# A two-way hybrid layer (2-D attention and mLSTM): all large SBUF tiles start at multiples of 64 bytes

## The chip, the cores and the metric

The kernel runs on one core of one Trainium2 chip. The metric is the device time of one execution in microseconds (us). TensorE multiplies matrices (PE in the profile, its weight loads PEld), VectorE (DVE) and ScalarE (ACT) work elementwise, GpSimd (POOL) fills constants and does small steps, SyncE (SP) issues most of the DMA transfers. SBUF is the on-chip memory: 128 partitions, in each of which a tile takes the same range of bytes. Where that range starts is what this change is about.

## The reference

One layer of a bidirectional encoder on 1,280 tokens (a prompt of 1,024 and a sample of 256) of 2,048 features, in fp32:

```python
hn = rmsnorm(x, norm_w)
proj = jnp.einsum('btd,dp->btp', hn, w_in)            # 2048 -> 9232 columns
# group A: 8 heads of neighbourhood attention over a grid 64 wide
att = neighbourhood_attention(q, k, v, rpb) * silu(na_g)
# group B: conv + SiLU on q and k, 4 heads of a chunkwise mLSTM in both directions
h = bidirectional_mlstm(silu(conv(mq)), silu(conv(mk)) * d**-0.5, mv, gates)
mem = rmsnorm(h, head_norm_w) * sigmoid(ml_o) * silu(ml_z)
y = rmsnorm(x + concat([att, mem]) @ w_out, final_norm_w)
```

## The kernel before

Every large fp32 matrix product is made of three matmuls: each operand is split into a rounded part hi and a rest lo (the helper `split`, lines 178 to 187: ACT casts hi, DVE subtracts for lo), and hi x hi, hi x lo and lo x hi are summed in PSUM. On top of this the projections and the out-projection use schemes with seven block products where a plain one has eight, so sums of blocks are formed on DVE and POOL ahead of them.

The work goes through these stages, with their place in the profiled execution:

- 0 to 1090 us, group A of the tokens (768 of them): `first_tiles` loads and splits x, then `pair_a` projects pairs of 128 columns with matmuls of 384 columns (`mm_c`, line 288; moving tiles xb and xg, weights such as A22s), and `unit_vg` makes v and gate columns (line 499).
- 1090 to 1365 us, group B (512 tokens): `proj_v` (line 777, 256 columns, the moving tile is the split weight wsv and the split x tiles x_0h, x_0l and so on are the stationary weights), the gates, and ten runs of `pair_s` (line 1416, 256 columns, 7 steps each of 8 x 3 matmuls; moving are x tiles in the steps 1, 2, 3 and block sums xs in the steps 6, 5, 4, 7; the weights S32s and the like come from the pool wb for the first half of each step and from xs2 for the second).
- 1365 to 2150 us, attention (lines 807 to 956, scores 810, transposes through ident 827, weights times v 923, 932, 938) and mLSTM (lines 1093 to 1330, matmuls 1132), interleaved with the rest of `proj_pair` (line 694, 512 columns, moving x, weights ws) and `proj_v`.
- 2150 to 2540 us, the out-projection `product` (line 1684, 512 columns, moving wo or wt, weights mo), the residual and the final norm (lines 1604 to 1668).

The tiles come from pools. A pool hands out one ring of equal slots per tag. Pools that are opened on the left grow up from the low end of SBUF (const, then xa and wa for group A; later late, xp1, xs2, and ap or "att" with mp), pools with `side="right"` grow down from the high end (xr for group A; later wb, xp0). A tile's size is rounded up to 32 bytes, and pools follow each other without gaps. So a pool's start depends on the sizes of all that was opened on its side before it. Before the change the constants take a number of bytes that is 32 past a multiple of 64, and the high end lies 32 past one as well. Most slots have sizes that are multiples of 64, so nearly everything starts at 32 of 64. The exceptions are five tags with an odd size in 32 bytes: po (520 floats, 2,080 bytes, six slots in wb, lines 657 to 658), sc (520, line 1385), sml (260, 1,040 bytes, line 802), and kvf and cb (516, line 1135). Their slots alternate between 0 and 32. Each of these tiles is used through views that are narrower than or as wide as the tile.

The order on each engine is not written by hand everywhere. A scheduler with an estimated timeline of its own sets it from priorities and from when slots come free; in the interleaved stage, where several streams are ready at once, small differences of its estimate change which stream's instruction comes next.

Of the kernel before, what the change touches and what calls it, by code (L numbers as in the profile page):

```python
# [9 lines left out]
F32 = mybir.dt.float32  # L10
F32R = mybir.dt.float32r
# [3 lines left out]
P = 128  # L15
# [14 lines left out]
NRA, NWS, NWT, NPC, NPO = 3, 8, 4, 5, 6  # L30
# [18 lines left out]
def kernel(  # L49
# [17 lines left out]
    nc = tc.nc  # L67
    V, S, G, PE, DM = nc.vector, nc.scalar, nc.gpsimd, nc.tensor, nc.sync

    const = ctx.enter_context(tc.tile_pool(name="const", bufs=1))  # L70
    dram = ctx.enter_context(tc.tile_pool(name="spill", bufs=1, space=bass.MemoryType.DRAM))
    ps = ctx.enter_context(tc.tile_pool(name="ps", bufs=3, space=bass.MemoryType.PSUM))

# [95 lines left out]
    def x_split(raw, k, g):  # L169
        h, l = x_pair(k, f"x{g}_{k}")  # L170
        S.mul(h, raw, lnw_sb[:, k : k + 1])
        V.scalar_tensor_tensor(
            l, raw, lnw_sb[:, k : k + 1], f(h), op0=ALU.mult, op1=ALU.subtract
        )
        return h, l
# [458 lines left out]
    for i, n1 in enumerate(order):  # L634
# [4 lines left out]
        k = i - 4  # L639
# [7 lines left out]
    wb, xp0 = pools  # L647
# [7 lines left out]
    xp1 = ctx.enter_context(tc.tile_pool(name="xp1", bufs=1))  # L655

    def po(name):
        return wb.tile([P, 520], F32, tag="po", name=name, bufs=NPO)

    def w_piece(src, name):  # L660
        raw = wb.tile([P, 1024], F32, tag="wraw", name=f"wr_{name}", bufs=2)
# [12 lines left out]
    def conv_b(o, ct):  # L674
        cv = po(f"pcv{ct}")
        yield from conv_taps(cv, o, ct, 516, 0)
        hi = wb.tile([P, 520], F32R, tag="po", name=f"pch{ct}", bufs=NPO)
        store_conv(ct, cv, hi, o, ((0, 258, GA - 2), (260, 516, TP)))

    FORTH = ((0, 1), (0, 0), (1, 0))  # L680
# [1 line left out]
    def proj_pair(n1, X, late=False):  # L682
        pb = [bank("pr", f"pc{n1}_{j}") for j in range(2)]
        for r in range(4):
            raw = w_piece(w_in[n1 // 2, r], f"{n1}_{r}")
            t = [w_split(raw, j * 512, j * 512 + 512, f"{n1}_{r}{j}") for j in range(2)]
            for f_ in range(2):
                for q in range(2):
                    xs = X.get(8 * f_ + 2 * r + q)
                    c = (2 * f_ + q) * P  # L690
                    first, last = r + f_ + q == 0, r == 3 and f_ == 1 and q == 1
                    for j, passes in enumerate((FORTH, FORTH[::-1])):
                        for m, (wi, xi) in enumerate(passes):
                            PE.matmul(  # L694
                                pb[j], t[j][:, wi, c : c + P], xs[xi],
                                start=first and m == 0, stop=last and m == 2,
                            )
        out = []
        for j in range(2):
            o = po(f"pco{n1}_{j}")  # L700
            if QK0 <= n1 < OT0:
                ct = n1 - QK0 + j
                DM.dma_start(o[:, 0:4], qb[ct])
                for z in (260, 518):
                    G.memset(o[:, z : z + 2], 0.0)
                out_scaled(
                    o[:, 4:].rearrange("p (s c) -> p s c", s=2)[:, :, :256],
                    pb[j].rearrange("p (s c) -> p s c", s=2),
                    rbs[1].rearrange("p (s c) -> p s c", s=2), n1,
                )  # L710
                for _ in conv_b(o, ct):
                    pass
                continue
            o = o[:, :GB]
            out_scaled(o, pb[j], rbs[1], n1)
            if n1 < GT0:
                store_qk(
                    n1 + j, o,
                    lambda dt: wb.tile([P, 520], dt, tag="po", name=f"ps{n1}_{j}_{dt}", bufs=NPO),
                    PARTS_B,  # L720
                )
            elif not late:
                DM.dma_start(pT[n1 + j][:, GA:], o)
            out.append(o)
        return out
# [20 lines left out]
    def proj_v(u, X):  # L746
        gates = u == NA_H // 2
        w = 272 if gates else 256
        nt = GB // P
        if gates:  # L750
            outs = [bank("a", f"pv{u}_{i}")[:, :w] for i in range(nt)]
        else:
            pb = [bank("pr", f"pv{u}_{i}") for i in range(nt // 2)]
            outs = [pb[t // 2][:, (t % 2) * 256 : (t % 2) * 256 + 256] for t in range(nt)]
        for r in range(4):
            raw = w_piece(w_in[NCH // 2 + u, r], f"v{u}_{r}")
            rawv = raw.rearrange("p (j f q c) -> p f q j c", j=2, f=2, q=2)
            if gates:
                graw = wb.tile([P, 2, 2, 16], F32, tag="wgr", name=f"wg{r}", bufs=2)
                DM.dma_start(  # L760
                    graw, w_g.rearrange("p (f r q c) -> p f r q c", f=2, r=4, q=2)[:, :, r]
                )
            for f_ in range(2):
                t = wb.tile([P, 2, 544], F32R, tag="wsp", name=f"wsv_{u}_{r}_{f_}", bufs=4)
                t4 = t[:, :, : 2 * w].rearrange("p h (k c) -> p h k c", k=2)
                h2, l2 = (
                    t4[:, z, :, 0:256].rearrange("p q (j c) -> p q j c", j=2) for z in range(2)
                )
                split(h2, l2, rawv[:, f_])
                if gates:  # L770
                    split(t4[:, 0, :, 256:272], t4[:, 1, :, 256:272], graw[:, f_])
                for tt in range(nt):
                    for q in range(2):
                        first, last = r + f_ + q == 0, r == 3 and f_ == 1 and q == 1
                        xh, xl = X.get(8 * f_ + 2 * r + q)
                        for m, (xs, wi) in enumerate(((xh, 0), (xh, 1), (xl, 0))):
                            PE.matmul(  # L777
                                outs[tt],
                                xs[:, tt * P : (tt + 1) * P],
                                t[:, wi, q * w : (q + 1) * w],  # L780
                                start=first and m == 0 and (gates or tt % 2 == 0),
                                stop=last and m == 2 and (gates or tt % 2 == 1),
                            )
        rc = rcs[1]
        for tt in range(nt):
            o = wb.tile([P, 520], F32R, tag="po", name=f"vo{u}_{tt}", bufs=NPO)
            o = o[:, :512].rearrange("p (a d) -> p a d", a=2)
            store_v(u, GA + tt * P, o, outs[tt][:, :256], rc[:, tt : tt + 1])
            if gates:
                V.scalar_tensor_tensor(  # L790
                    gt[:, GA // P + tt, :], outs[tt][:, 256:272], rc[:, tt : tt + 1], gb_sb,
                    op0=ALU.mult, op1=ALU.add,
                )
# [5 lines left out]
        return ap.tile([P, 512], dt, tag="mid", name=name, bufs=6)[:, :n]  # L799

    def sml(name, n=256, dt=F32):
        return ap.tile([P, 260], dt, tag="sml", name=name, bufs=6)[:, :n]

    def na_tile(tag, shape, name, bufs, dt=F32):
        return ap.tile(shape, dt, tag=tag, name=name, bufs=bufs)
# [287 lines left out]
    def ml_units(sq, h, gates):  # L1093
# [38 lines left out]
                PE.matmul(o, lhs(a_), rhs(b_), start=first and m == 0, stop=last and m == 2)  # L1132

        def kvt(name, tag="kvf", bufs=4):
            t = ap.tile([P, 516], F32, tag=tag, name=name, bufs=bufs)
            return t.rearrange("p (t c) -> p t c", c=VW)

        def c_split(name, src):
# [193 lines left out]
    class LazyX:  # L1332
# [2 lines left out]

        def get(self, k):
            if k not in self.t:
                self.t[k] = x_split(x_raw(wb, 520, "po", NPO, 1, k), k, 1)
            return self.t[k]

    def run(*streams):
# [37 lines left out]
    def pair_s(n1, tag, bg):  # L1379
# [2 lines left out]
        x0, y0, z0, y1, z1 = bx[:, :256], by[:, :256], bz[:, :256], by[:, 256:], bz[:, 256:]  # L1382
        conv = QK0 <= n1 < OT0
        off = (4, 262) if conv else (0, 256)
        Cn = [xs2.tile([P, 520], F32, tag="sc", name=f"{nm}c0", bufs=2), po(f"{nm}c1")]
        c0, c1, c2, c3 = (Cn[j][:, o : o + 256] for j in range(2) for o in off)
        steps = (
            (1, x0, True), (2, y0, True), (6, x0, False), (5, z0, True), (3, z1, False),
# [62 lines left out]
    def finish_s(n1, Cn):  # L1451
        for j, o in enumerate(Cn):
            if QK0 <= n1 < OT0:
                ct = n1 - QK0 + j
                DM.dma_start(o[:, 0:4], qb[ct])
                for z in (260, 518):
                    G.memset(o[:, z : z + 2], 0.0)
                yield from conv_b(o, ct)
                continue
            o = o[:, :GB]  # L1460
            if n1 < GT0:
                store_qk(
                    n1 + j, o,
                    lambda dt: wb.tile([P, 520], dt, tag="po", name=f"S{n1}_{j}_{dt}", bufs=NPO),
                    PARTS_B,
                )
                yield
                continue
            if OT0 <= n1 < ZT0:
                S.activation(o, o, AF.Tanh, scale=0.5)  # L1470
            elif n1 >= GT0:
                th = po(f"S{n1}th{j}")[:, :GB]
                S.activation(th, o, AF.Tanh, scale=0.5)
                V.scalar_tensor_tensor(o, th, 1.0, o, op0=ALU.add, op1=ALU.mult)
            DM.dma_start(pT[n1 + j][:, GA:], o)
            yield
# [391 lines left out]
```

## Time and profile before

| quantity | value |
|---|---|
| time, median of 3 runs | 2541.99 us (2541.35 to 2542.15) |
| span of the profiled execution | 2540.0 us, mean TensorE clock 0.999 |
| PE busy | 2523.1 us, 99% of the span, 15,197 matmuls |
| DVE, ACT, POOL busy | 1980.9 us (78%), 1348.3 us (53%), 597.7 us (24%) |
| DMA | 505.67 MB, mean 199 GB/s |

The profiled execution has no time of its own beside its span; the median of the runs is 2.0 us above the span. A row of the page's groups gives the line of the kernel, the engine, the operation, the tile written and those read, the shape and the count, then busy us in all and the mean ns of one. Matmuls are pipelined: one lasts longer than the spacing from its start to the next one's, and the busy us of a group count overlapped time once, so busy us over count is about that spacing.

### The profile page before, as it was taken

The page shows a single profiled execution, that of the slowest core. Times are in us where ns is not written, and L with a number is a line of the kernel's source. Part 1 is how long each engine was busy: PE and PEld are TensorE (multiplying, and loading weights), DVE is VectorE, ACT ScalarE, POOL GpSimd, SP SyncE. Part 2 cuts the span into 40 slices and gives each one's busy share as a digit, 9 for nine tenths or more (in the row PEclk, how much of TensorE's full clock was granted, in tenths as well). Part 3 has the DMA queues.
Part 4 walks back from the last instruction along what each step waited for, and adds up shares of the span by engine and source line. Part 5 has one row for each costly group of instructions (what it writes and reads, how often), then busy time and mean ns, then how long its engine had stood idle before and what let it go on. Part 6 is the DMA issues. An engine that isn't in the chain of part 4 may idle for free.

```text
span 2540.0 us, 44864 instructions
## 1 busy us (share of the span) xinstructions
PE 2523.1 (99%) x15197; PEld 2363.7 (93%) x15197; DVE 1980.9 (78%) x4034; ACT 1348.3 (53%) x3052; POOL 597.7 (24%) x883
## 2 busy tenths in 40 slices
PE   9999999999999999999999999999999999999998
PEld 9999999999999999999999899899998888888887
DVE  8787878898879798898875676775875665889696
ACT  8644455444444444475655666666665653344445
POOL 0553555544444454400000011010100103000002
PEclk9999999999999999999999999999999999999999
DMA  6563464546434342467778878878977849546327
GB/s 218 171 206 122 140 215 146 183 130 201 152 112 130 100 140 89 151 229 221 230 249 279 263 265 290 284 252 274 300 219 246 287 125 355 198 146 208 95 87 257
DMA packets 308189, 505.67 MB, mean 199 GB/s; under 512 B 49040, under 2 KB 195000, under 8 KB 307960
## 3 DMA queue, kind: packets, MB, share of 16 engines
q1 hardware_dynamic: 304856, 490.75, 60.0%
q0 software_dynamic: 2960, 11.80, 1.2%
q8 instruction: 120, 1.97, 0.3%
q14 instruction: 109, 0.89, 0.1%
q10 hardware_dynamic: 144, 0.26, 0.0%
HBM read 374.18 MB, written 128.52 MB: 198 GB/s over the span
## 4 chain that ended last, share of the span: by engine, by line
PE 87%; DMA 2%; DVE 2%; issue 0%; ACT 0%; POOL 0%; SPq 0%; POOLq 0%; ACTq 0%; DVEq 0%
PE pc L694 16%; PE po L1684 15%; PE pv L777 5%; PE A22b L288 1%; PE A44b L288 1%; PE A14b L288 1%; PE A18b L288 1%; PE A10b L288 1%; PE A48b L288 1%; PE A52b L288 1%; PE A50b L288 1%; PE A42b L288 1%; PE A20b L288 1%; PE A16b L288 1%; PE A12b L288 1%; PE A70b L288 1%
## 5 line engine op out<-in xcount | busy, mean ns | idle before, releaser
L1684 PE MATMUL po<-wo,mo 128*128 128x512 f32 (+1 forms) x1620 | 374.2, 392 | 0.0
L1684 PEld LDWEIGHTS po<-wo,mo 128*128 128x128 f32 x1620 | 303.3, 188 | 70.1
L180 DVE TENSOR_TENSOR ws<-wr,ws 128x512 fp32r<-128x512 f32 x144 | 97.9, 690 | 40.4 <-ACT ws L179 38.0
L179 ACT CAST ws<-wr 128x512 fp32r<-128x512 f32 x144 | 87.5, 617 | 64.9 <-PE pc L694 56.3
L179 ACT CAST mo<-mb 128x640 fp32r<-128x640 f32 x72 | 52.0, 726 | 108.8 <-PE po L1684 96.2
L120 POOL TENSOR_SCALAR rs<-rs 128x1 f32<-128x1 f32 x9 | 4.2, 468 | 370.4 <-DVE rs L1637 367.2
L180 DVE TENSOR_TENSOR mo<-mb,mo 128x640 fp32r<-128x640 f32 x72 | 58.4, 817 | 32.2 <-ACT mo L179 32.1
L1605 DVE TENSOR_TENSOR y<-y,po 128x512 f32<-128x512 f32 x89 | 57.2, 680 | 13.5 <-PE po L1684 13.3
L179 ACT CAST mo<-ms 128x640 fp32r<-128x640 f32 x40 | 28.9, 725 | 51.9 <-PE po L1684 30.6
L180 DVE TENSOR_TENSOR wsv<-wr_v,wsv 128x512 fp32r<-128x512 f32 x64 | 44.6, 702 | 12.5 <-ACT wsv L179 12.2
L179 ACT CAST wsv<-wr_v 128x512 fp32r<-128x512 f32 x64 | 38.9, 616 | 23.1 <-PE pv L777 13.5
L430 DVE SCALAR_TENSOR_TENSOR pcv<-pco,cw_sb,pcv 128x516 f32<-128x516 f32 x48 | 36.1, 753 | 7.7 <-ACT pcv L424 7.7
L180 DVE TENSOR_TENSOR mo<-ms,mo 128x640 fp32r<-128x640 f32 x40 | 32.7, 816 | 10.7 <-ACT mo L179 10.7
L1118 POOL MEMSET mls_0v<- 128x2 f32 x4 | 0.4, 102 | 163.4 <-DVE S_dt.float L180 139.0
L1619 ACT ACTIVATE jk<-y 128x512 f32<-128x512 f32 x39 | 24.5, 629 | 26.0 <-DVE y L1605 25.6
L133 ACT ACTIVATE xq<-xq 128x1024 f32<-128x1024 f32 x20 | 21.2, 1062 | 29.6 <-DMA xq<-in_xtok_dram 25.1
L288 PE MATMUL fb<-xg,fw 128*128 128x384 f32 x192 | 34.7, 335 | 0.2 <-ACT xg L186 0.2
L288 PEld LDWEIGHTS fb<-xg,fw 128*128 128x128 f32 x192 | 33.3, 188 | 0.5 <-ACT xg L186 0.5
L1568 DVE TENSOR_TENSOR ms<-mb,mb 128x640 f32<-128x640 f32 x40 | 32.6, 815 | 0.0
L815 DVE CUSTOM_DVE_ANT_0 nap_0st<-nap_0s,nap_0bt 128x384 f32<-128x384 f32 x32 | 17.7, 553 | 17.4 <-PE nap_0s L810 6.7
L818 ACT ACTIVATE nap_0st<-nap_0st,nap_0sm 128x384 f32<-128x384 f32 x32 | 19.7, 616 | 21.4 <-DVE nap_0sm L815 21.4
L265 DVE TENSOR_TENSOR pco<-pc,rstdb 128x512 f32<-128x512 f32 x28 | 19.1, 685 | 14.2 <-PE pc L694 14.0
(2770 smaller groups left out, 8507.2 us busy)
## 6 DMA issues: line engine op xcount, KB each, us to landing
wr<-in_w_in_dram SPq DMA_DIRECT2D x72, 512.0 KB, 4.9
wr_v<-in_w_in_dram SPq DMA_DIRECT2D x32, 512.0 KB, 4.6
wb<-in_w_o_dram SPq DMA_DIRECT2D x48, 256.0 KB, 3.4
xq<-in_xtok_dram SPq DMA_DIRECT2D x20, 512.0 KB, 4.3
mb<-mx POOLq DMA_DIRECT2D x32, 320.0 KB, 7.8
y<-in_xtok_dram SPq DMA_DIRECT2D x35, 256.0 KB, 5.3
wr_wp<-in_w_o_dram SPq DMA_DIRECT2D x16, 512.0 KB, 6.5
vS<-vo SPq DMA_DIRECT2D x24, 256.0 KB, 5.5
```

Of the source, the lines that this page charges most:

```text
L133: S.activation(raw, raw, AF.Square, accum_out=ssq[g][:, t, q : q + 1])
L179: S.copy(hi, src)
L180: return V.tensor_tensor(lo, src, f(hi), op=ALU.subtract)
L288: PE.matmul(o, w(a_), x(b_), start=first and m == 0, stop=last and m == 2)
L430: V.scalar_tensor_tensor(dst[:, a:n], src[:, a + j - pad : n + j - pad], cw_sb[:, ct, j : j + 1], dst[:, a:n], op0=ALU.mult, op1=ALU.add,)
L694: PE.matmul(pb[j], t[j][:, wi, c : c + P], xs[xi], start=first and m == 0, stop=last and m == 2,)
L777: PE.matmul(outs[tt], xs[:, tt * P : (tt + 1) * P], t[:, wi, q * w : (q + 1) * w], start=first and m == 0 and (gates or tt % 2 == 0), stop ...
L818: S.activation(st, st, AF.Exp, bias=sm[:, 0:1], scale=-1.0, accum_out=sm[:, 2:3])
L1568: V.tensor_tensor(t, x, y_, op=op)
L1605: V.tensor_tensor(Y[p, q, tt], Y[p, q, tt], bk, op=op)
L1619: S.activation(jk, Y[p, q, tt], AF.Square, accum_out=ss[t][:, c : c + 1])
L1684: PE.matmul(bk[tt] if o is None else o, m[xi][:, tt * P : (tt + 1) * P], w[wi][:, cs], start=first and kk == 0 and j == 0, stop=last and j ...
```

## The change

It puts small padding tiles at both ends of SBUF and widens the rows of the five odd-sized tags to the next multiple of 64 bytes:

```diff
     const = ctx.enter_context(tc.tile_pool(name="const", bufs=1))
+    top = ctx.enter_context(tc.tile_pool(name="top", bufs=1, side="right"))
+    G0 = nc.gpsimd
+    for pool, n in ((const, 24), (top, 24)):
+        G0.memset(pool.tile([P, n], F32, tag="line", name=f"line{n}"), 0.0)
...
     def po(name):
-        return wb.tile([P, 520], F32, tag="po", name=name, bufs=NPO)
+        return wb.tile([P, 528], F32, tag="po", name=name, bufs=NPO)[:, :520]
...
     def sml(name, n=256, dt=F32):
-        return ap.tile([P, 260], dt, tag="sml", name=name, bufs=6)[:, :n]
+        return ap.tile([P, 272], dt, tag="sml", name=name, bufs=6)[:, :n]
...
         def kvt(name, tag="kvf", bufs=4):
-            t = ap.tile([P, 516], F32, tag=tag, name=name, bufs=bufs)
+            t = ap.tile([P, 528], F32, tag=tag, name=name, bufs=bufs)[:, :516]
...
-        Cn = [xs2.tile([P, 520], F32, tag="sc", name=f"{nm}c0", bufs=2), po(f"{nm}c1")]
+        Cn = [xs2.tile([P, 528], F32, tag="sc", name=f"{nm}c0", bufs=2), po(f"{nm}c1")]
```

The other places where a po tile is made directly (conv_b, proj_pair, proj_v, finish_s, LazyX) get 528 in the same way. A padding tile has 24 floats, 96 bytes, so it moves the pools behind it by 96 bytes: from 32 of 64 to 0. The views keep the old widths, so no instruction works on more data. The constants in const lie behind the padding tile too, and they move by 96 bytes as well: ident starts at 1,152 before (a multiple of 64) and at 1,248 after (32 past one).

The instructions are the same on every engine except for two more memsets on POOL. They stand at POOL's start, between the program's branch and the identity matrix. Before:

```order
L1863 UNCONDITIONAL_BRANCH
masks.py:197 MEMSET ident 128x128
L101 MEMSET ones 128x128
L112 MEMSET mhalf 128x16
masks.py:199 ISA
```

After (line numbers of the code behind the new lines grow by 4):

```order
L1867 UNCONDITIONAL_BRANCH
L74 MEMSET line_61 128x24
L74 MEMSET line_63 128x24
masks.py:197 MEMSET ident 128x128
L105 MEMSET ones 128x128
```

The fills of ident, ones and mhalf come two memsets later. On PE the order is the same up to about 1680 us; from there to about 2150 us, in the interleaved stage, instructions move by some rows. The first such place, at the end of a unit of `proj_v` (pv) with the mLSTM of head 1 of the prompt (mlp_1acc and mlp_1in are its PSUM results, mlp_1p the weighted scores, mlp_1Cf the state, mlp_1q the queries). Before:

```order
L777 MATMUL pv_1_18077<-wsv_2_0_18192,x_5h 128x256
L1132 MATMUL mlp_1acc_21942<-mlp_1v,mlp_1p_21763 128x258 x3
L777 MATMUL pv_1_18077<-wsv_2_0_18192,x_5h 128x256
L777 MATMUL pv_1_18077<-wsv_2_0_18192,x_5l 128x256
L777 MATMUL pv_1_18077<-wsv_2_0_18192,x_4h 128x256 x2
L777 MATMUL pv_1_18077<-wsv_2_0_18192,x_4l 128x256
L777 MATMUL pv_1_18077<-wsv_2_0_18192,x_5h 128x256 x2
L1132 MATMUL mlp_1in_21947<-mlp_1Cf,mlp_1q 128x258 x6
L777 MATMUL pv_1_18077<-wsv_2_0_18192,x_5l 128x256
```

After:

```order
L1136 MATMUL mlp_1acc_21949<-mlp_1v,mlp_1p_21770 128x258 x3
L781 MATMUL pv_1_18084<-wsv_2_0_18199,x_4h 128x256
L781 MATMUL pv_1_18084<-wsv_2_0_18199,x_4l 128x256
L781 MATMUL pv_1_18084<-wsv_2_0_18199,x_5h 128x256 x2
L781 MATMUL pv_1_18084<-wsv_2_0_18199,x_5l 128x256
L781 MATMUL pv_1_18084<-wsv_2_0_18199,x_4h 128x256 x2
L781 MATMUL pv_1_18084<-wsv_2_0_18199,x_4l 128x256
L781 MATMUL pv_1_18084<-wsv_2_0_18199,x_5h 128x256 x2
L781 MATMUL pv_1_18084<-wsv_2_0_18199,x_5l 128x256
L781 MATMUL pv_0_18083<-wsv_2_1_18226,x_12h 128x256 x2
L781 MATMUL pv_0_18083<-wsv_2_1_18226,x_12l 128x256
```

mlp_1acc moves ahead by three matmuls of `proj_v`, and mlp_1in, which followed seven matmuls after it, now comes behind the start of the next unit half. A second place lies about 90 rows on, in `proj_pair` (pc) with the mLSTM of head 2. Before:

```order
L694 MATMUL pc_0_18320<-x_2h,ws_10_18356 128x512 x2
L694 MATMUL pc_0_18320<-x_3l,ws_10_18356 128x512
L694 MATMUL pc_0_18320<-x_3h,ws_10_18356 128x512 x2
L1132 MATMUL mlp_2in_22117<-mlp_2Cf,mlp_2q 128x258 x6
L694 MATMUL pc_1_18321<-x_0h,ws_01_18327 128x512 x2
```

After:

```order
L698 MATMUL pc_0_18327<-x_2h,ws_10_18363 128x512 x2
L698 MATMUL pc_1_18328<-x_0h,ws_01_18334 128x512 x2
L698 MATMUL pc_1_18328<-x_0l,ws_01_18334 128x512
L698 MATMUL pc_1_18328<-x_1h,ws_01_18334 128x512 x2
L698 MATMUL pc_1_18328<-x_1l,ws_01_18334 128x512
L698 MATMUL pc_1_18328<-x_8h,ws_01_18334 128x512 x2
L698 MATMUL pc_1_18328<-x_8l,ws_01_18334 128x512
L698 MATMUL pc_1_18328<-x_9h,ws_01_18334 128x512 x2
L698 MATMUL pc_1_18328<-x_9l,ws_01_18334 128x512
L698 MATMUL pc_1_18328<-x_2h,ws_11_18366 128x512
L1136 MATMUL mlp_2in_22124<-mlp_2Cf,mlp_2q 128x258 x6
```

mlp_2in now comes after 13 matmuls of pc_1, and three of pc_0 that stood ahead of it come later.

More of the change, by code (lines that the diff above doesn't have):

```diff
@@ L676, in conv_b @@
         yield from conv_taps(cv, o, ct, 516, 0)
-        hi = wb.tile([P, 520], F32R, tag="po", name=f"pch{ct}", bufs=NPO)
+        hi = wb.tile([P, 528], F32R, tag="po", name=f"pch{ct}", bufs=NPO)
         store_conv(ct, cv, hi, o, ((0, 258, GA - 2), (260, 516, TP)))
@@ L718, in proj_pair @@
                     n1 + j, o,
-                    lambda dt: wb.tile([P, 520], dt, tag="po", name=f"ps{n1}_{j}_{dt}", bufs=NPO),
+                    lambda dt: wb.tile([P, 528], dt, tag="po", name=f"ps{n1}_{j}_{dt}", bufs=NPO),
                     PARTS_B,
@@ L785, in proj_v @@
         for tt in range(nt):
-            o = wb.tile([P, 520], F32R, tag="po", name=f"vo{u}_{tt}", bufs=NPO)
+            o = wb.tile([P, 528], F32R, tag="po", name=f"vo{u}_{tt}", bufs=NPO)
             o = o[:, :512].rearrange("p (a d) -> p a d", a=2)
@@ L1337, in get @@
             if k not in self.t:
-                self.t[k] = x_split(x_raw(wb, 520, "po", NPO, 1, k), k, 1)
+                self.t[k] = x_split(x_raw(wb, 528, "po", NPO, 1, k), k, 1)
             return self.t[k]
@@ L1463, in finish_s @@
                     n1 + j, o,
-                    lambda dt: wb.tile([P, 520], dt, tag="po", name=f"S{n1}_{j}_{dt}", bufs=NPO),
+                    lambda dt: wb.tile([P, 528], dt, tag="po", name=f"S{n1}_{j}_{dt}", bufs=NPO),
                     PARTS_B,
```

## The prediction

> **What bounds the kernel now.** I read the clock first, then the page's busy shares and its chain, then the windows by stage, then the list of what TensorE waited for. The clock row and the head of the page:
>
> ```profile
> core 0: 2540.0 us, clock 0.999
> ```
>
> ```profile
> span 2540.0 us, 44864 instructions
> PE 2523.1 (99%) x15197; PEld 2363.7 (93%) x15197; DVE 1980.9 (78%) x4034; ACT 1348.3 (53%) x3052; POOL 597.7 (24%) x883
> PE 87%; DMA 2%; DVE 2%; issue 0%; ACT 0%; POOL 0%; SPq 0%; POOLq 0%; ACTq 0%; DVEq 0%
> ```
>
> The clock is granted nearly in full, so no change in power can give time back. PE is busy for 2523.1 of 2540.0 us and carries 87% of the chain that ended last. The windows, with the columns of their first line, show that this holds in each stage:
>
> ```profile
> core 0: us, PE busy (x) PEld busy (x) DVE busy (x) ACT busy (x) POOL busy (x), PEclk, DMA share, GB/s
> 0.00:10.00 10.00, 7.64 (x31) 7.32 (x32) 3.05 (x7) 5.81 (x12) 0.87 (x8) 1.00 0.70 206
> 320.00:1090.00 770.00, 770.00 (x4470) 768.23 (x4469) 653.01 (x1172) 369.52 (x885) 370.53 (x414) 1.00 0.47 148
> 1300.00:1680.00 380.00, 379.33 (x2724) 356.76 (x2723) 270.31 (x686) 232.85 (x562) 31.97 (x124) 1.00 0.83 271
> 1680.00:2150.00 470.00, 469.15 (x2788) 415.29 (x2787) 306.55 (x821) 261.22 (x639) 57.04 (x165) 1.00 0.77 255
> 2150.00:2540.00 390.00, 381.70 (x1675) 310.67 (x1673) 313.17 (x492) 172.41 (x316) 13.76 (x21) 0.99 0.52 170
> ```
>
> From 320 to 1090 us PE has no idle time; in the interleaved stage, 1300 to 2150 us, it has 0.67 + 0.85 = 1.5 us. The longest entries of PE's own waits:
>
> ```profile
> engine line waited for: us in total, times, longest us
> PE A26b L288 <- DVE gt L517: 1.8, 1, 1.8
> PE fb L342 <- DVE idle L340: 1.4, 1, 1.4
> PE pv L777 <- DVE wsv L180: 1.0, 2, 0.8
> PE nas_0s L810 <- DMA nas4qk<-qS: 0.8, 1, 0.8
> PE nap_0s L810 <- DMA nap3qk<-kS: 0.6, 1, 0.6
> ```
>
> No feeder holds PE for 2 us. So the time is a sum of matmul spacings, and the change can act in two ways only: it makes a matmul's own reads shorter or longer, or it opens new waits.
>
> **The change part by part.** It moves addresses. As the two programs place their tiles, 3,839 of 4,234 SBUF tiles begin 32 bytes past a multiple of 64 before and 395 on it; after, 4,162 of 4,236 lie on it, and the 74 others are constants (the identity among them, which goes from 0 to 32) and scratch of 16 to 32 bytes. The instructions are the same but for two memsets.
>
> *The two memsets* stand first on POOL and delay ident, ones and mhalf. The nearest row is mhalf's, 16 columns wide against 24:
>
> ```profile
> 0.79 1.28 ACT L338 ACT_TABLE_LOAD   x1 [0.79 <-PEq L1853]
> 0.93 0.20 POOL L101 MEMSET ones<- 128x128 f32 x1
> 1.07 0.11 POOL L112 MEMSET mhalf<- 128x16 f32 x1
> 2.08 0.20 ACT L338 ACTIVATE mhalf<-ones 128x1 f32<-128x1 f32 x1
> ```
>
> Two of them cost 2 x 0.11 = 0.22 us. The first reader of ones is ACT at 2.08, after its table load; mhalf ends at 1.18, so 0.22 us more leave 0.7 us of cover. Queued behind them are POOL's identity steps, whose transposes come much later. I take 0; without the cover it would be 0.2 us.
>
> *The matmuls' moving reads.* Does a read that begins in the middle of a 64-byte piece cost anything? The trace of before has matmuls of 256 columns whose moving tile already lies at 0 (the attention's weights npt, line 932), others at 32 (wsv, line 777) and others at 96 of 128 (the sums xs, line 1416). The first two rows below give minimum, median and maximum in ns, the rest busy us and mean ns:
>
> ```profile
> L932 PE MATMUL nap_0o<-nap_0pt,nap_0v x48: 277/281/285, 1425.8 to 2047.1; 128*128 128x256 f32 x48
> ...
> L777 PE MATMUL pv<-wsv,x_0h x64: 274/282/384, 1088.8 to 1829.3; 128*128 128x256 f32 x56, 128*128 128x272 f32 x8
> ```
>
> ```profile
> L1416 PE MATMUL S32bx<-xs,S32s 128*128 128x256 f32 x48 | 5.8, 276 | 0.0
> L1416 PE MATMUL S32bx<-x_1h,S32s 128*128 128x256 f32 x2 | 0.4, 286 | 0.0
> L1416 PE MATMUL S32bx<-x_0h,S32s 128*128 128x256 f32 x2 | 0.4, 282 | 0.0
> L1416 PE MATMUL S32bx<-x_6h,S32s 128*128 128x256 f32 x2 | 0.4, 282 | 0.0
> ```
>
> ```profile
> L1684 PE MATMUL po<-wo,mo 128*128 128x512 f32 x1608 | 372.8, 393 | 0.0
> L288 PE MATMUL A22b<-xg,A22s 128*128 128x384 f32 x144 | 26.8, 339 | 0.0
> L288 PE MATMUL A58b<-xg,A58s 128*128 128x384 f32 x144 | 25.6, 334 | 0.0
> ```
>
> At 0 the median is 281 ns, at 32 it is 282: 1 ns. The shortest, 276, lies at 96, which is 32 past a multiple of 64 as well. So the aligned moving read brings nothing that the trace shows. What the trace does not show is a stream with both operands on the multiple of 64, since npt's partner, the attention's v, is at 32. I bound it from both sides. Below: every matmul gets the short spacing of line 1416, 282 - 276 = 6 ns less, 15,197 x 0.006 = -91 us. Above: every matmul goes from 282 to the longest of these, 286, 15,197 x 0.004 = +61 us. I take 0, by the row nearest to the case, line 932 (one operand on the line, 1 ns).
>
> The Trainium skill, TensorE: Matmul & The Clock Gate, section Back-to-back issue gap, gives an isolated warm matmul N/2.4 + 2.5 ns, so 216 ns for 512 columns. The row of line 1684 gives 372.8/1608 = 232 ns, 16 more. If that excess were the mid-piece start, the sum by that section would fall by some 200 us, as an estimate. Line 932, whose moving tile starts on such a multiple, speaks against it.
>
> *The pairs of line 1416* are the one place where spacing hangs on addresses. Ten pairs run there, each 7 steps of 24 matmuls: 96 with xs and 72 with x tiles. Fast ones have the moving tile at 96 of 128 and weights at 32; x_0 and x_1 lie at 32 with weights at 32 and take 282 to 286, and x_6, at 96, is still slow just behind such. After the change the xs tiles lie at 64, and the weights at 0 (even halves, from wb) and at 64 (odd halves, from xs2). If an equal place within 128 is what slows, half of the 96 turn slow: 48 x 10 x 0.006 = +2.9 us, while the x tiles go on with half of theirs equal. Ends: all 72 fast, 72 x 10 x 0.006 = -4.3; all 96 slow, +5.8. Line 777 speaks for a weak rule (282 for tiles at 32 whatever x's place), so I take a third of 2.9: +1.0 us.
>
> *DVE and ACT* read and write tiles that move from 32 to 0. Tiles of 2080 bytes in one ring already alternate between 0 and 32 (po, line 265):
>
> ```profile
> L265 DVE TENSOR_TENSOR pco<-pc,rstdb x28: 668/689/693, 1422.3 to 2143.2; 128x512 f32<-128x512 f32 x28
> ```
>
> All 28 lie within 25 ns, 4%, whichever slot they have. DVE is busy 306.6 of 470 us in that stage; 4% of that, 12 us, would fall beside PE either way. 0.
>
> *DMA.* Transfers now start at multiples of 64. The queues' share and the largest load:
>
> ```profile
> q1 hardware_dynamic: 304856, 490.75, 60.0%
> wr<-in_w_in_dram SPq DMA_DIRECT2D x72, 512.0 KB, 4.9
> ```
>
> Against PE's 0.8 + 0.6 us of waits for DMA above, even 5% more on a load (0.25 us of 4.9) is hidden by the ring of buffers. 0; bound +1 us. The Trainium skill, DMA: Bandwidth & Descriptors, section How a descriptor splits into AXI transactions, says that a transfer off a 256-byte boundary also fetches the unused bytes below its start. By it the change costs some 1 to 2% of beats (before, most starts lie 32 past such a boundary; after, often 64, 128 or 192), an estimate that speaks against the change; no run here shows those beats.
>
> *The order.* PE's order is the same to about 1680 us; in the rest of the interleaved stage some 900 of 15,186 instructions trade places with neighbours, the projections' (lines 694 and 777) with those of the mLSTM (line 1132) and of the attention. PE idles 0.85 us in that window, so there is next to nothing to gain and a wait or two to lose (one of the listed waits is 0.8): -0.5 to +3 us. At the second place shown with the change, mlp_2in comes behind 13 matmuls of proj_pair more and 3 fewer: 10 x 0.232 us (512 columns, row of line 1684) = 2.3 us later. Its readers are ACT and DVE, and DVE is free for 470 - 306.6 = 163 us of this stage, so they take it up when it comes, and PE has proj_pair's matmuls meanwhile. I take 0.
>
> **Sum.** 2540.0 + 0 + 0 + 1.0 + 0 + 0 + 0 = 2541.0 us of span. The median of the runs is 2541.99, 2.0 above the span of the profiled execution, which has no separate time; that lies around the span. Forecast 2541.0 + 2.0 = 2543.0 us. A measurement of this kernel can tell 0.2%, 5 us, from no change: 0.33 ns for each matmul.
>
> **The rivals.**
>
> *Both operands aligned, short spacing everywhere.* Each matmul gives 6 ns back: 2543 - 91 = 2452 us. For it: the 276 ns rows show that the 282 are not a floor, and never do both operands of a long stream lie on the line. Against it: line 932. Chance 0.08. The Trainium skill (TensorE: Matmul & The Clock Gate, Back-to-back issue gap) would put this case lower still.
>
> *A small gain per matmul.* Aligned operands save 0.5 to 1.7 ns, the step between 282 and 281 or a little more: 15,197 x 0.0005 to 0.0017 = 8 to 26 us, 2517 to 2535. For it: lines 932 and 777 differ by 1 ns in this direction, and the two forms of line 288 by 5 without visible reason. Chance 0.24.
>
> *Slower: equal places collide.* The change brings nearly all tiles to 0 or 64 of 128, and weights of pair stage and x tiles meet at the same one more often. If the slow spacing needs equal places and persists, as behind x_1, all 96 xs matmuls of each pair turn slow and the x tiles reach 286: 5.8 + 72 x 10 x 0.004 = +8.7, with the sum's +1.0 in it, 2550.7 us. It decides from some 60% of the xs matmuls on. If it spreads to the long streams of lines 288, 694 and 1684 as well it costs up to +61, 2603. Chance 0.14 and 0.03. Against it: line 777 has equal places now, at 282, like line 932 with unequal ones.
>
> *Slower: the new order opens waits.* After 1680 us a delayed pair of mLSTM matmuls makes DVE late, which frees PSUM late; five waits of 1.2 us give +6, 2549. Chance 0.06. It decides from 5 us of idle in that window; before has 0.85.
>
> *It does not do what it says.* 74 tiles stay at 32, among them ident, the moving operand of all transposes, which loses its place at 0. At 1 ns each that is under 1 us, so it stays inside the forecast.
>
> **How the numbers follow.** Forecast within 5 us of now: 0.45. Faster: 0.08 + 0.24 = 0.32. Slower: 0.14 + 0.03 + 0.06 = 0.23. The range goes from 2517, the lower end of the small gain, to 2551, the upper end of the collisions; it leaves out 0.08 below and 0.03 above, and some 0.08 of tails. The forecast's own range is 2537 to 2547.
>
> **What would show it.** Right: line 932 at 281 ns, L1684 at 393, xs rows of line 1416 between 276 and 280, PE idle between 1680 and 2150 us under 2 us, POOL's first memsets early by 0.2 us without ACT's 2.08 moving. Wrong: L1684 or L694 off by more than 1 ns (small gain), near 387 (full gain); xs rows at 282 or more (collision); PE waits for DVE or DMA above 5 us in the order's stage.

## The result and the profile after

The changed kernel takes 2545.7 us (median of 20 runs, 2543.68 to 2550.07) against 2542.17 us before (20 runs, 2540.62 to 2544.91). The ratio is 1.0015 with an interval of 1.0008 to 1.0022. That is 3.5 us more: less than the 5 us that the prediction called no change, but not noise. The forecast was 2543.0 us.

The clock row and the head of the page of the changed kernel:

```profile
core 0: 2544.1 us, clock 0.998
```

```profile
span 2544.1 us, 44858 instructions
PE 2527.4 (99%) x15197; PEld 2369.3 (93%) x15197; DVE 1983.9 (78%) x4034; ACT 1348.4 (53%) x3052; POOL 596.1 (23%) x885
PE 86%; DVE 2%; DMA 2%; issue 0%; ACT 0%; SPq 0%; POOLq 0%; POOL 0%; ACTq 0%; DVEq 0%
```

PE is busy 4.3 us longer for the same 15,197 matmuls, and the span is 4.1 us longer. So the time went into matmuls, not into waits. PE's longest waits confirm this:

```profile
engine line waited for: us in total, times, longest us
PE fb L292 <- ACT xg L190: 1.9, 1, 1.9
PE A26b L292 <- DVE gt L521: 1.6, 1, 1.6
PE fb L346 <- DVE idle L344: 1.4, 1, 1.4
PE nap_0s L814 <- DMA nap6qk<-kS: 1.2, 1, 1.2
```

The next question is which line's matmuls. The windows view can be narrowed to one line of the kernel; its row then gives PE's busy time of that line and the number of its instructions. Between 1160 and 1370 us this is the whole of `pair_s`, ten pairs of 168 matmuls. First line 1416 of the kernel before, then its twin, line 1420, of the changed kernel:

```profile
1160.00:1370.00 210.00, 194.35 (x1680) 1.00 0.72 225
```

```profile
1160.00:1370.00 210.00, 198.73 (x1680) 1.00 0.70 218
```

These 1,680 matmuls take 198.73 - 194.35 = 4.38 us more. That is the whole difference of the spans, 4.1 us. One pair, looked at by form, shows how. The rows are those of the changed kernel; before, the first of them stood at 5.8 us and 276 ns:

```profile
L1420 PE MATMUL S32bx<-xs,S32s 128*128 128x256 f32 x48 | 5.9, 279 | 0.0
L1420 PE MATMUL S32by<-xs,S32s 128*128 128x256 f32 x24 | 3.1, 280 | 0.0
L1420 PE MATMUL S32bz<-xs,S32s 128*128 128x256 f32 x24 | 3.0, 279 | 0.0
```

And with minimum, median and maximum (before 276/276/276 for the same pair):

```profile
L1420 PE MATMUL S32bx<-xs,S32s x48: 274/278/287, 1194.0 to 1202.2; 128*128 128x256 f32 x48
```

Before, every one of the 48 took exactly 276 ns. Now they lie between 274 and 287.

The rest of the profile hardly moved. Only line 932 fell a little: the median of nap_0o from 281 to 277 ns, the busy time of all 192 of the line from 27.9 to 27.5 us. The attention's line 932 is now 936, the long streams 1684 and 288 are now 1688 and 292:

```profile
L936 PE MATMUL nap_0o<-nap_0pt,nap_0v x48: 276/277/287, 1430.4 to 2045.6; 128*128 128x256 f32 x48
...
L781 PE MATMUL pv<-wsv,x_0h x64: 274/281/386, 1089.5 to 1833.3; 128*128 128x256 f32 x56, 128*128 128x272 f32 x8
```

```profile
L1688 PE MATMUL po<-wo,mo 128*128 128x512 f32 x1608 | 372.3, 393 | 0.0
L292 PE MATMUL A22b<-xg,A22s 128*128 128x384 f32 x144 | 26.6, 337 | 0.0
L292 PE MATMUL A58b<-xg,A58s 128*128 128x384 f32 x144 | 25.6, 334 | 0.0
```

At the start the two memsets take 0.17 us together, and ACT's first instruction on ones still starts at 2.08 us:

```profile
0.79 0.17 POOL L74 MEMSET line<- 128x24 f32 x2 [0.29 <-POOLq L1857]
1.04 0.20 POOL L105 MEMSET ones<- 128x128 f32 x1
1.19 0.11 POOL L116 MEMSET mhalf<- 128x16 f32 x1
2.08 0.20 ACT L342 ACTIVATE mhalf<-ones 128x1 f32<-128x1 f32 x1
```

The interleaved stage, where the order changed, runs from the last matmul of `pair_s` to the first of `product`. By the starts of these in the two traces it took 1361.96 to 2142.95 us before, 781.0 us, and 1365.92 to 2147.48 after, 781.6 us.

### The profile page after: what moved, and what is told of

Same layout as the page of the kernel before. It is cut to its first block, busy times and chain, and to the rows that moved or that the text cites. A ratio compares the mean times of both kernels' runs of the same rounds, so it can differ in the third digit from the quotient of the medians.

```text
span 2544.1 us, 44858 instructions
## 1 busy us (share of the span) xinstructions
PE 2527.4 (99%) x15197; PEld 2369.3 (93%) x15197; DVE 1983.9 (78%) x4034; ACT 1348.4 (53%) x3052; POOL 596.1 (23%) x885
## 3 DMA queue, kind: packets, MB, share of 16 engines
q1 hardware_dynamic: 304856, 490.75, 60.1%
## 4 chain that ended last, share of the span: by engine, by line
PE 86%; DVE 2%; DMA 2%; issue 0%; ACT 0%; SPq 0%; POOLq 0%; POOL 0%; ACTq 0%; DVEq 0%
PE po L1688 15%; PE pc L698 15%; PE pv L781 5%; PE A14b L292 1%; PE A52b L292 1%; PE A48b L292 1%; PE A18b L292 1%; PE A44b L292 1%; PE A22b L292 1%; PE A10b L292 1%; PE A20b L292 1%; PE A16b L292 1%; PE A46b L292 1%; PE A42b L292 1%; PE A12b L292 1%; PE A50b L292 1%
## 5 line engine op out<-in xcount | busy, mean ns | idle before, releaser
L184 DVE TENSOR_TENSOR wsv<-wr_v,wsv 128x512 fp32r<-128x512 f32 x64 | 43.8, 690 | 11.6 <-ACT wsv L183 11.3
L503 PE MATMUL vg<-vgs,xg 128*128 128x272 f32 x216 | 28.8, 288 | 0.0
```

What stands on the lines that cost most here:

```text
L184: return V.tensor_tensor(lo, src, f(hi), op=ALU.subtract)
L503: PE.matmul(banks[z, tt], xop(i, kk, xi)[:, tt * P : (tt + 1) * P], t[:, wi], start=kk == 0 and i in (1, 3) and m == 0, stop=kk == 7 and i ...
```

## The theory and its rivals

**Theory (halves).** What counts in `pair_s` is not whether a tile starts on a multiple of 64 bytes, but where the moving tile and the weights stand against each other within 128 bytes. In the trace of before, a matmul of 256 columns with xs, whose operands start in opposite 64-byte halves, takes 276 ns and mostly follows the last one by 113 to 114 ns; those in the same half take about 282, with a mean spacing of 119. As the two programs place the tiles, 1,260 of the 1,680 had opposite halves before the change and 540 have them after it: 480 with xs, and 60 with x_4 and x_5, which the expectations below leave out of their count. In `pair_s` the two operands stand either 0 or 64 bytes apart within 128 in every run of the layer, so `pair_s` alone cannot tell "in opposite halves" from "64 bytes apart".

**Rivals.** The multiple of 64 itself is bad for this line. Or the new order of the interleaved stage costs the time, and `pair_s` is a bystander.

## The experiments

**Only the second halves of the weights moved back.** The edit moves the weight slots of xs2 by 64 bytes. All operands of `pair_s` stay on multiples of 64, and PE's order is that of the changed kernel, instruction for instruction.

```diff
     proj_pair(QT0, X)
     operand_sums()
+    G.memset(xs2.tile([P, 16], F32, tag="pad", name="pad_w"), 0.0)
```

> The changed kernel with one more padding tile of 64 bytes in xs2 ahead of its weight slots. It moves only the second halves of the pair stage's weights, from 64 of 128 bytes to 0; xs stays at 64, everything stays on multiples of 64. Theory (halves): a matmul of pair_s has a spacing of 113 to 114 ns where its moving tile and its weights start in opposite 64-byte halves of 128 bytes, and about 119 where they start in the same half. By it 1,260 of the 1,680 matmuls are opposite again as before the change (480 in the changed kernel), all xs rows are at 276 ns, the stage from the first to the last matmul of line 1416 takes 195.6 us as before (changed kernel 200.0), and the time is 2541.5 to 2542.5 us. Rival (the multiple of 64 itself costs it): the stage stays at 200 us and the time at 2545.7. Rival (the new order of the interleaved stage costs it): the stage may change, the time stays above 2545.

Measured: 2542.43 us against 2541.9, ratio 0.9999 (0.9990 to 1.0008). The expectations give a stage as the stretch from the first to the last matmul of the line, other lines' matmuls between them included (195.6 us before); the rows give the busy time of the line alone (194.35 us before). The row of line 1420:

```profile
1160.00:1370.00 210.00, 194.91 (x1680) 1.00 0.71 224
L1420 PE MATMUL S32bx<-xs,S32s x48: 276/276/276, 1194.6 to 1202.7; 128*128 128x256 f32 x48
```

64 bytes under one ring of weights bring 3.8 of the 4.4 us back, and all 48 are at 276 ns again. The first rival expected the stage to stay at 200 us, the second a time above 2545; both fall.

**All operands in opposite halves.** In addition a pool of 64 bytes between wb and xp0:

```diff
-        for name, bufs in (("wb", 2), ("xp0", 1)):
+        for name, bufs in (("wb", 2), ("gap", 1), ("xp0", 1)):
             pools.append(ctx.enter_context(tc.tile_pool(name=name, bufs=bufs, side="right")))
+        G.memset(pools[1].tile([P, 16], F32, tag="gap", name="pad_x"), 0.0)
...
-    wb, xp0 = pools
+    wb, _, xp0 = pools
```

> As the run before, and in addition a pool of 64 bytes between wb and xp0, so that all x tiles start at 64 of 128 and all weights of pair_s and proj_pair at 0: all 1,680 matmuls of pair_s, all 1,728 of proj_pair and all 1,440 of proj_v have operands in opposite halves. Theory (halves): pair_s gains 420 x 5.5 ns = 2.3 us more than before the change, its stage takes 193.3 us. If the halves decide in the other streams too, the 1,080 + 900 matmuls that are turned there gain up to 5.5 ns each, 11 us: 2529 us. If they decide in pair_s only, 2540 us. Rival (the multiple of 64, or the order): 2545 us or more.

Measured: 2539.79 us against 2541.9, ratio 0.9992 (0.9983 to 1.0001). Its row for `pair_s`, line 1421 here:

```profile
1160.00:1370.00 210.00, 191.82 (x1680) 1.00 0.74 230
```

`pair_s` gains 2.5 us on the kernel before, near the 2.3 expected; the time itself is not clear of the kernel before, since its interval reaches 1.0001. The other question was whether the halves decide in the other streams too. They don't. PE's order is that of the changed kernel, so that is the one to compare with. First `proj_pair`, line 698, of the changed kernel, where 648 of the 1,728 are opposite, then line 699 of this run, where all are:

```profile
1080.00:2160.00 1080.00, 441.47 (x1728) 1.00 0.78 256
```

```profile
1080.00:2160.00 1080.00, 442.20 (x1728) 1.00 0.78 258
```

The 512-column stream is 0.7 us slower where 5.9 us faster had been thinkable (1,080 x 5.5 ns), and `proj_v` stands at 200.8 and 201.0 us. In the kernel before the two lines take 439.7 and 203.0 us. That difference goes with the order, not with the halves: the four runs with the changed kernel's order have 441.1 to 442.2 and 200.8 to 201.1 us, the three with the order of before 439.7 to 439.9 and 202.6 to 203.0, whatever their places. The two nearly cancel, so the run lands on the "in pair_s only" branch, 2540 us.

**Widened rows without padding.** The change without its `top` pool and its two padding tiles: everything at 32 past a multiple of 64, PE's order exactly that of the changed kernel.

> The change without its two padding tiles: the rows of the odd tags are widened, everything lies at 32 past a multiple of 64 as before, PE's order has the length of the changed kernel's. All 1,680 matmuls of pair_s have both operands at 96 of 128, in the same half. Theory (halves): all are slow, 1,260 x 5 ns = 6.3 us more than before the change, the stage of line 1416 takes about 202 us, the time is 2548. Rival (the multiple of 64 itself costs it): none lies on one, so the stage takes 195.6 us and the time is 2542. Rival (the new order costs it): the stage is as before, the time 2545 to 2546.

Measured: 2548.06 us against 2541.9, ratio 1.0026 (1.0018 to 1.0035).

```profile
1160.00:1370.00 210.00, 200.58 (x1680) 1.00 0.69 216
L1416 PE MATMUL S32bx<-xs,S32s x48: 274/282/288, 1194.3 to 1202.7; 128*128 128x256 f32 x48
```

This is the slowest of all, with no tile of the streams on a multiple of 64: 6.2 us more in `pair_s`, 6.2 us more in the time. All operands are at 96 of 128, in the same half. The widened rows change where the pools behind them start, and here they put both operands into the same half everywhere. The new order, on the other hand, is free: from the last matmul of `pair_s` to the first of `product` it takes 780.3 us, before 781.0.

**Padding without widened rows.** The two padding tiles alone; PE's order is that of the kernel before.

> The change's two padding tiles alone, rows as wide as before: PE keeps the order of before up to its line numbers, nearly all matmul operands lie on multiples of 64. 840 matmuls of pair_s have operands in opposite halves, 840 in the same. Theory (halves): 420 fast ones are lost, 2.1 us, the stage of line 1416 takes 197.7 us, the time is about 2544. Rival (the new order costs it): 2542. Rival (the multiple of 64 itself costs it): 200 us of stage and 2545.7.

Measured: 2545.05 us against 2541.9, ratio 1.0013 (1.0005 to 1.0022).

```profile
1160.00:1370.00 210.00, 199.02 (x1680) 1.00 0.69 218
```

The direction is right, the size is not: 4.7 us instead of 2.1. From its first to its last matmul the stage takes 200.3 us, and with 2545 us this is what the first rival expected (200 us and 2545.7). So this run does not speak against the multiple of 64; the run with all operands opposite (191.8 us on multiples of 64) and the one before this (200.6 us off them) do. The 840 opposite matmuls did not run at 114 ns: their mean spacing in this trace is 116 to 117. In this placement the half changes with each half of a step, and behind each change some matmuls are slow, as x_6 was in the trace before. So the count of opposite matmuls gives the best case, and how often the half changes belongs to the price.

**The kernel before with the 64-byte gap alone.** The gap pool of the second experiment put into the kernel before; nothing else. All operands are opposite, none on a multiple of 64 that was not there before.

> The kernel before with one edit: a pool of 64 bytes between wb and xp0, so that the ten x tiles of xp0 go from 32 to 96 of 128 bytes; nothing lies on a multiple of 64 that did not before. All 1,680 matmuls of pair_s have operands in opposite halves (1,260 before). Theory (halves): the stage of line 1416 takes 193.1 us as in the run with all operands opposite (before 195.6), the time is 2539.5 us. Rival (on multiples of 64 the opposite halves are faster, off them not): 195.6 us of stage, 2542 us.

Measured: 2540.46 us against 2541.77, ratio 0.9996 (0.9987 to 1.0005).

```profile
1160.00:1370.00 210.00, 192.80 (x1680) 1.00 0.74 228
```

`pair_s` gains 1.6 of the expected 2.5 us, off the multiples of 64. In the time this is within its interval. Its stage of 194.0 us lies between the theory's 193.1 and the rival's 195.6, nearer to the theory. The missing 1 us against the run with all opposite stands in a few places: in this trace 223 of the 1,680 spacings are 116 ns or more, in that run 49, all in the first pair. 174 x 5 ns are 0.9 us. As the program places the tiles, the moving tiles of xp0 start 224 bytes past a multiple of 256, those of xp1 and the sums xs 96 past one: the same half of 128, but 128 bytes apart within 256. The moving tile changes between the two places six times in each pair, and in the pairs 2 to 10 just there three spacings in a row are slow (means of 117, 122 and 118 ns): 161 of the 167 slow ones. In the run with all opposite every moving tile starts 192 past a multiple of 256, there is no such change, and the pairs 2 to 10 have no slow spacing. So the place within 256 bytes does not decide whether a stream is fast, but a change of it has its price.

**Streams that lie still.** Three kernels leave out the layer and run streams of 96 matmuls from tiles that don't move, with nothing beside them. The core of the first, where `place` gives the shift of the moving tile:

```python
for kk in range(8):
    q, k = divmod(kk, 4)
    o = place(kk)
    for m, (wi, xi) in enumerate(passes):
        PE.matmul(b[:, :n], W[q][:, wi, k * P : (k + 1) * P], X[kk][:, xi, o : o + n], ...)
```

> Leaves out the whole layer and writes zeros to the outputs; it runs fifteen streams of 96 matmuls from tiles that lie still: weights at 0 of 128 bytes, moving tiles shifted by 0, 32, 64 or 96 bytes. Names: a is the order of pair_s (lo, hi, hi moving against weights hi, hi, lo), v that of proj_v (moving hi, lo, hi), b a repeat, then the columns, then the shift; alt changes between 0 and 64 from block to block. Theory (halves): a256at64 has 276 ns and a spacing of 113, a256at0 about 282 and 119, a256at32 and at96 lie between; a256alt is nearer to slow, since a change of half was followed by some slow matmuls. For 384 and 512 columns, and for v256, the traces showed no dependence: equal rows at 0 and 64. Rival (it is the distance of the tiles or the work beside, not the half): the same mean at 0, 32, 64 and 96. Rival (a multiple of 64 for both is what counts): at0 and at64 alike and faster than at32 and at96.

Its windows of the four streams a256at32, a256at64, a256at96 and b256at0 are cut where one stream's first matmul starts and the next one's does, so the width is the time of a stream; the count takes in matmuls of the neighbours that reach into the window:

```profile
46.50:58.00 11.50, 11.50 (x99) 1.00 0.00 1
58.00:69.30 11.30, 11.30 (x98) 1.00 0.01 1
69.30:80.80 11.50, 11.50 (x99) 1.00 0.01 1
80.80:92.10 11.30, 11.30 (x99) 1.00 0.00 0
```

The theory as it stood failed here: at 64 and at 0 the stream takes the same 11.3 us for 96 matmuls, 118 ns each. At 32 and 96, which were to lie between, it is 11.5, 119 to 120 ns. The streams of 384 and of 512 columns were alike at 0 and 64 within 3 ns, as expected. These streams differ from `pair_s` in one thing, among others, that the theory had left out: the moving tile's lo part lay 2,176 bytes behind hi, in `pair_s` 2,048. The second kernel takes the distances of `pair_s`; "wide" keeps 2,176:

```python
w, x = wv(kk, wi, ws, 0, P), xv(kk, xi, zs, o, n)   # zs, ws: floats from hi to lo
```

> Leaves out the whole layer and writes zeros to the outputs; streams of 96 matmuls as in the run of streams before, but with the distances of pair_s: lo of a moving tile lies 2048 bytes behind hi (2176 there), lo of the weights 2176 behind hi. In the first run of streams the half made no difference (118 ns at 0, 118 at 64), against the theory as it stood. Theory mended (halves, where the moving parts lie a multiple of 256 bytes apart, so that all moving tiles of a stream keep the same place): pair64b has 113 to 114 ns, pair0b and pair128b 118 to 119, pair192b 113 to 114 if only the half counts; wide0b and wide64b (2176 apart) both 118 as in the first run; even (weights 2048 apart) as pair. long (512 columns) and mid (384 columns, 1536 apart) equal at 0 and 64, as in the kernel's traces. vee (weights and moving exchanged, as proj_v) equal at 0 and 64. Rival (the work beside on DVE, ACT and DMA makes it): all streams of 256 columns at 118 whatever the place.

By form, with busy us and mean ns of one:

```profile
L111 PE MATMUL pair0b<-XB,WB 128*128 128x256 f32 x96 | 11.8, 282 | 0.0
L111 PE MATMUL pair64b<-XB,WB 128*128 128x256 f32 x96 | 11.6, 280 | 0.0
L111 PE MATMUL pair96b<-XB,WB 128*128 128x256 f32 x96 | 11.8, 284 | 0.0
L111 PE MATMUL pair128b<-XB,WB 128*128 128x256 f32 x96 | 11.5, 281 | 0.0
L111 PE MATMUL wide64b<-XB,WB 128*128 128x256 f32 x96 | 11.5, 280 | 0.0
L111 PE MATMUL pair192b<-XB,WB 128*128 128x256 f32 x96 | 11.0, 276 | 0.0
```

Half a hit: a shift of 192 bytes gives the 276 ns of the kernel, with nothing beside the stream, so work on DVE, ACT and DMA is not what makes it. But 64, in the same half as 192, stays slow, also with the weights' parts 2,048 bytes apart (even64b, 11.5 us and 279 ns). A shift of 96 is in the opposite half as well, and pair96b is among the slowest. So what allows the short spacing looks like a distance of 64 bytes within 128 rather than the half as such; one stream at 96 does not show it. Whether the period is longer than 128 bytes, or whether the stream had only not settled, that is, not fallen into the even spacing of 113 to 114 ns, the third kernel asks. Its streams "one" use one weights tile throughout, "two" alternate between two as the second kernel's:

```python
def stream(nm, n, o, qs=(0,)):      # qs: the weights tiles in turn
```

> Leaves out the whole layer and writes zeros to the outputs; streams of 96 matmuls as in the second run of streams, where only the shift of 192 bytes was fast (113 ns) and 64 was not (119). one: all 96 matmuls of a stream use one weights tile (four blocks of 128 columns) and four moving tiles; two: two weights tiles in turn, 4,352 bytes apart, as in pair_s; long: 512 columns. Theory (opposite halves are fast once settled, and a change of weights tile unsettles them for some matmuls, as in the kernel's traces where 3 to 9 slow ones stand at the start of a step): one64b, one192b, one320b and one448b at 113 to 114, one0b, one128b, one256b and one384b at 118 to 119; two64b slower than one64b. Rival (the place within 256 or 512 bytes counts, not the half): one64b stays at 118 to 119, one192b at 113, and 320 and 448 tell which period. long: 231 to 234 at every shift.

```profile
L106 PE MATMUL one64b<-XB,WB 128*128 128x256 f32 x96 | 11.0, 276 | 0.0
L106 PE MATMUL one128b<-XB,WB 128*128 128x256 f32 x96 | 11.5, 281 | 0.0
L106 PE MATMUL one192b<-XB,WB 128*128 128x256 f32 x96 | 11.1, 276 | 0.0
L106 PE MATMUL one256b<-XB,WB 128*128 128x256 f32 x96 | 11.6, 282 | 0.0
L106 PE MATMUL one320b<-XB,WB 128*128 128x256 f32 x96 | 11.0, 276 | 0.0
L106 PE MATMUL one448b<-XB,WB 128*128 128x256 f32 x96 | 11.1, 276 | 0.0
L106 PE MATMUL two64b<-XB,WB 128*128 128x256 f32 x96 | 11.0, 276 | 0.0
L106 PE MATMUL two320b<-XB,WB 128*128 128x256 f32 x96 | 11.6, 280 | 0.0
```

With one weights tile the rule is clean: 276 ns at 64, 192, 320 and 448, 281 to 285 at 0, 128, 256 and 384. Over these shifts, in steps of 64, the period is 128 bytes. With two weights tiles there are two outcomes: two64b is fast, where slower than one64b was expected, and so are two192b and two448b (276 ns each); two320b is not. And two64b has the same addresses and the same sequence as pair64b above, which was slow. They differ in the stream ahead of them and in the PSUM bank that they write, and they ran on different chips; two320b ran beside two64b on one chip. So a distance of 64 bytes within 128 allows the short spacing, and a stream whose weights change place may or may not fall into it. The streams of 512 columns stayed at 231 to 233 ns at every shift, as expected.

## Why the prediction was right, point by point

- **No gain from aligned reads** (chance of a gain 0.32): right. Line 1684 is at 393 ns before and after, line 288's A58b at 334. With both operands on multiples of 64, which no stream in the trace of before had, these rows became no faster. Line 932, which the prediction wanted at 281 ns, has 277 in the row of nap_0o; its operands went from 32 to 64 bytes apart, and 0.4 us for the line is all of it. The run with widened rows, off the multiples of 64 and also 64 apart, has 27.6 us there too, but shares the new order, so the cause of this small gain stays open. The 200 us that the Trainium skill's formula for an isolated matmul (TensorE: Matmul & The Clock Gate, Back-to-back issue gap) would have allowed were not there; even in the short spacing matmuls of 256 columns start 113 to 114 ns apart (one64b), where the formula has 109.
- **The memsets**: right. 0.17 us for 0.22, and nobody late.
- **DVE, ACT, DMA**: right. The DMA queue's share went from 60.0 to 60.1%, and PE's waits for DMA stay near 1 us each. The Trainium skill's rule on transfers off a 256-byte boundary (DMA: Bandwidth & Descriptors, How a descriptor splits into AXI transactions) was not visible in the time, and no run here shows it.
- **The order**: right, and now shown. The run with widened rows has the changed kernel's order and loses nothing behind `pair_s`. PE was idle for 470 - 468.59 = 1.4 us between 1680 and 2150 us, under the 2 us that the prediction named.
- **The pairs of line 1416**: the mechanism was right, the term was mis-sized. The prediction took "a third of 2.9: +1.0 us"; it measured 4.4. The rule gave 480 xs matmuls that turn slow. The x tiles do not "go on with half of theirs equal", as the prediction put it: 300 of their 720 were opposite before, 60 are after. So 480 + 240 = 720 more stand in the same half, and at 119 instead of 114 ns that is 3.6 us. The other 0.8 us fit the xs matmuls that stayed opposite but now stand between same-half ones: their mean spacing went from 114.0 to 115.6 ns, 480 x 1.6 = 0.8 us. The reason for taking only a third was line 777, which is at 282 ns wherever its tiles are. That was read as weakness of the rule. The streams show a reason why it can stay slow without weakening it: its moving tiles are the split weights, whose hi and lo lie 2,176 bytes apart, so that their place within 256 shifts by 128 at each change between hi and lo, and in the stream "wide" 64 was no faster than 0 at that distance. That the distance is the reason is not shown: pair64b was slow without it. The time still fell within 2537 to 2547, the forecast's own range, because the term is small against it and not because it was well sized.
- **The rival "equal places collide"** was this same mechanism with its full price, 8.7 us. Its "point from which it decides", 60% of the xs matmuls, was not reached: 50% turned.

Open: why a 256-column stream settles in one case and not in the other, whether the half or the distance of 64 bytes is what counts, and why 384 and 512 columns don't show it at all.

## What to carry to other kernels

Rounding every tile to a multiple of 64 bytes is not a gain by itself; here it put operands that are read together into the same half of 128 bytes, where before they stood apart. Look for matmul groups whose minimum, median and maximum are the same number, as 276/276/276 here: such a stream was settled in these runs, and a change of a tile ahead of it in a pool could unsettle it. Where such a term is small against the bound of the measurement, read it from the busy time of its own line in a window: there the five edits lie between 191.8 and 200.6 us, one trace each, and are easily told apart, while the intervals of several of their times overlap.

## What the runs showed of the hardware

- A matmul of 256 columns has a settled spacing of 113 to 114 ns (11.0 us for 96, one64b) where moving tile and weights start 64 bytes apart within 128 bytes, and 118 to 119 on average where they start at the same place (one128b 11.5 us for 96; all of `pair_s` in the run with widened rows).
- A moving tile that changes its place within 256 bytes by 128 was followed by three slow spacings (means of 117, 122 and 118 ns, in the run with the gap alone); with lo 2,176 bytes behind hi instead of 2,048, which makes such a change at every step between hi and lo, the mean stayed at 280 ns (wide64b).
- A stream can stay in either state: with the same addresses and the same sequence all 96 matmuls took 276 ns in two64b, and 277 to 285 in pair64b, on another chip.
- Matmuls of 384 and 512 columns showed no such dependence: line 288 (384) takes 1041.8 us with 2,916 of its 5,928 in opposite halves (before) and with none (weights moved back); `proj_pair` (512) 441.1 us with none of 1,728 (widened rows) and 442.2 with all.
